# Moving the transposed activations and branch outputs by 32 bytes modulo 256 in a hybrid decoder trunk

## The chip, the core and the metric

The kernel runs on one core of a Trainium2 chip. The metric is device time in microseconds of one execution. TensorE (PE) multiplies, with a separate weight-load stream (PEld); VectorE (DVE), ScalarE (ACT) and GpSimd (POOL) do the elementwise work; SyncE (SP) issues most transfers.

## The reference

Two layers. Each has a parallel mixer (an mLSTM branch and a gated DeltaNet branch, both fed by one input projection), a gated merge, an output projection and a layer norm, then a SwiGLU block and a second layer norm. Everything is float32, with 256 tokens and a model width of 1024.

```python
proj = einsum('bsd,dn->bsn', x, w_in)              # q, k, v, gates of both branches
ha = mlstm(...) ; hb = gated_delta(...)            # 4 heads of 128/256, 8 heads of 128
y = sigmoid(gate_a) * (ha @ w_branch_a) + sigmoid(gate_b) * (hb @ w_branch_b)
x = layernorm(ALPHA * x + y @ w_out)
gt, up = split(x @ w_ffn_up)                       # 2 x 2816 columns
x = layernorm(ALPHA * x + (silu(gt) * up) @ w_ffn_down)
```

## The kernel before

**Precision and matmuls.** Every large product is made from three float32r matmuls: each operand is held as a high part and a remainder (`xtH`/`xtL` for the activations, two halves of one tile for the weights), and high x high, high x low and low x high are summed in PSUM (`three`, L281; L304; L324). One instruction, `mm` at L279, issues them all, so the trace knows them by tile names. In an `out<-a,b` of L279 the moving operand (streamed) is the first of the two where the row has 256 columns and `xtH`, `xtL`, `haH` and so on lead; with 512 columns the weights move and the activations are loaded.

**Two forms.** `chunkB` (L377) loads a 128 x 128 block of the weight unit (`wR`) and streams 256 columns of the transposed activations; `chunkA`, `pairA` and `splitA` (L296, L312, L335) load a 128 x 128 block of the activations and stream 512 columns of the weight unit. The last pass of the last layer (`pieces=2`, L1172) streams weights in halves of 256 columns. Before each matmul stands its own weight load: 7,474 matmuls, 7,474 loads.

**Weight units.** Weights arrive in units of 128 x 1024 floats. `loading` (L233) puts a unit's high and low part side by side in one of six ring buffers `wR` (`SLOT` floats each, L49), or in a spot that is free for a while (`wT0` to `wT3`, `wh0` to `wh2`; `SPOTS`, L45). ACT makes the high part (L255), DVE the remainder (L256). `SHIFT` (L50) moves a unit inside its ring buffer; the units listed at L166 (va, oa, zb, up0, up1 and, in the last layer, dn1 from its fifth unit on, where they have no spot of their own) are shifted, the rest lie at its start.

**Where the operands lie.** The pools hand out addresses in the order in which tiles are made. Byte address in a partition modulo 256, from the built program:

| tile | role | modulo 256 |
|---|---|---|
| `xtH`, `xtL` | transposed activations | 128 |
| `haH`, `haL`, `hbH`, `hbL` | transposed outputs of the two branches | 128 |
| `wR`, unshifted; `wT*`, `wh*` | weight units | 192 |
| `wR`, shifted by 48 floats | weight units of the 512-column form | 128 |
| `yH`, `yL`, `hH`, `hL` | merged branches; SwiGLU activations | 192 |
| `wgH`, `wgL` | gate weights, 24 columns (96 bytes) for each of 8 blocks | 128 + 96 k |

Column slices are multiples of 512 bytes, so these hold for every matmul of a kind; for the gates the block k decides. In what follows the **offset** of a pair is the address of the loaded operand minus that of the streamed one, modulo 256: 64 for `xt`, `ha`, `hb` streamed against an unshifted unit, 0 where a shifted unit is streamed against `xt`, 0 for `yH` and `hH` with an unshifted unit or a spot, minus 64 where a spot is streamed against `xt`, and 64 where the shifted units of dn1 meet `hH`.

**Order.** PE's order is written out by hand (`PLAN`, L125: U is one unit of large matmuls, the other words are pieces of the branches). The other engines' order comes from a list scheduler in the file (`arrange`, L1217) with costs of its own, which knows no addresses.

Of the kernel before, what the change touches and what calls it, by code (L numbers as in the profile page):

```python
# [12 lines left out]
F32 = mybir.dt.float32  # L13
# [4 lines left out]
P = 128  # L18
# [19 lines left out]
def chunk_order():  # L38
    return ORDER + ["wb", "wo"] + [f"up{j}" for j in range(UP)] + ["dn0", "dn1"]
# [7 lines left out]
         ("va0", 0): "T0", ("va0", 1): "T1", ("va0", 2): "T2", ("va0", 3): "T3"}  # L47
WARM = 8
SLOT = 2 * UC + 64  # L49
SHIFT = 48  # L50
STEPS = (1, 4, 7, 10, 14, 18, 23, 30)
LN_LATE = (5, 6)
LATE = 8 * (UP - 3)
# [84 lines left out]
class Net:  # L138
    def __init__(self, ctx, tc, a, dbg=None):
        self.tc, self.nc, self.a, self.dbg = tc, tc.nc, a, dbg  # L140
        nc = tc.nc
        self.fix = ctx.enter_context(tc.tile_pool(name="fix", bufs=1))
        self.raw = ctx.enter_context(tc.tile_pool(name="raw", bufs=4))
        self.hl = ctx.enter_context(tc.tile_pool(name="hl", bufs=6))
        self.pj = ctx.enter_context(tc.tile_pool(name="pj", bufs=4, space=bass.MemoryType.PSUM))
        self.sm = ctx.enter_context(tc.tile_pool(name="sm", bufs=4, space=bass.MemoryType.PSUM))
        self.dr = ctx.enter_context(tc.tile_pool(name="dr", bufs=2, space=bass.MemoryType.DRAM))
        self.u = 0
        self.clock = 0
        self.due = []  # L150
        self.lnt = {}
        self.ahead = []
        self.ring = 0
        self.busy = set()
        self.F = None
        self.t3 = False
        self.spots = {}
        self.shift = {}
        n = 0
        for l in range(NL):  # L160
            for name in chunk_order():
                for i in range(COUNT.get(name, 4)):
                    spot = SPOTS.get((name, i))
                    if spot and (name != "va0" or l):
                        self.spots[n] = spot
                    elif name[:2] in ("va", "oa", "zb") or name in ("up0", "up1") or l == NL - 1 and name == "dn1" and i > 3:  # L166
                        self.shift[n] = SHIFT
                    n += 1
        fix = self.fix
        self.xt = [fix.tile([P, KT, S], F32R, name="xtH"), fix.tile([P, KT, S], F32R, name="xtL")]  # L170
        self.cst = fix.tile([P, 4 * P + 2 * S], F32, name="cst")
        c = self.cst
        self.idn = c[:, 0:P]
        self.tri = c[:, P:2 * P]
        self.one = c[:, 2 * P:3 * P]
        self.gm = c[:, 3 * P:4 * P]
        self.pm = c[:, 4 * P:4 * P + S]
        self.ei = c[:, 4 * P + S:4 * P + 2 * S]
        self.x = fix.tile([P, 2, D], F32, name="x")
        self.mh = fix.tile([P, 8], F32, name="mh")  # L180
        self.ph = fix.tile([P, 8], F32, name="ph")
        nc.gpsimd.memset(self.mh, -0.5)
        nc.gpsimd.memset(self.ph, 0.5)
        nc.vector.memset(self.x[:, 0, 0:P], 0.0)
        ps = self.sm.tile([P, 512], F32, name="sm")
        for i in range(WARM):
            self.mm(ps[:, 0:P], self.x[:, 0, 0:P], self.x[:, 0, 0:P], True, True)
# [758 lines left out]
    def mixer(self, l):  # L946
        nc, M, a = self.nc, self.M, self.a
        xt = self.xt
        mt = M.tile
# [9 lines left out]
            nc.gpsimd.memset(t, 0.0)  # L959
        st = [{}, {}]  # L960
        sm = {}
        self.gnc = mt([P, 16], F32, name="gnc")[:, 0:1]
        gates = self.gates(l, xt)
        cw = mt([P, 24, 4], F32, name="cw")
        self.gn = gn = mt([P, D], F32, name="gn", tag="vs", bufs=2)
# [447 lines left out]
```

## Time and profile before

| | us |
|---|---|
| median of three runs (1019.75 to 1020.79) | 1020.4 |
| the profiled execution | 1020.09 |
| its span, first to last instruction | 1018.3 |
| PE busy | 1006.9 |
| DVE busy | 734.8 |
| ACT busy | 595.6 |

An entry of the grouped views reads: line, engine, operation, out<-in tiles, shape, count, busy time, mean nanoseconds of one. Matmuls overlap: one of 256 columns lasts some 276 ns in its record while the next starts some 113 ns later. The distance from start to start is the pace that PE pays; the duration shows which pace a stretch ran at.

### The profile page before, as it was taken

How to read it: one execution, taken by the hardware profiler on the slowest of the kernel's cores; microseconds unless marked ns; L12 is line 12 of the kernel's file. 1: busy time of each engine (PE TensorE's matmuls, PEld its weight loads, DVE VectorE, ACT ScalarE, POOL GpSimd, SP SyncE). 2: the span in 40 equal slices, each digit the busy share in tenths (PEclk: the TensorE clock that was granted, in tenths of full speed). 3: DMA queues.
4: the chain of work that ended last, by engine and by line, in shares of the span. 5: the costliest groups of instructions: out<-in, count | busy, mean ns of one | idle time of the engine just before them, and what ended most of it. 6: DMA issues, size and time to landing. Idle time of an engine off the chain costs nothing.

```text
span 1018.3 us, 18926 instructions
## 1 busy us (share of the span) xinstructions
PE 1006.9 (99%) x7474; PEld 941.1 (92%) x7474; DVE 734.8 (72%) x1311; ACT 595.6 (58%) x1108; POOL 45.4 (4%) x68
## 2 busy tenths in 40 slices
PE   9999999999999999999999999999999999999997
PEld 7999999999998899998889999998999989999886
DVE  5788998799668655556647799878994885556453
ACT  5677567866655554455445865767667564445440
POOL 1000000100001000000010100001000010000001
PEclk9999999999999999999999999999999999999998
DMA  8876235645556666667644842555355666666641
GB/s 295 275 245 190 79 106 187 207 125 166 166 187 220 214 187 194 199 182 226 215 119 151 272 147 81 190 165 167 104 173 180 224 199 200 200 191 189 185 164 41
DMA packets 57400, 183.61 MB, mean 180 GB/s; under 512 B 6624, under 2 KB 14048, under 8 KB 56672
## 3 DMA queue, kind: packets, MB, share of 16 engines
q1 hardware_dynamic: 50688, 179.13, 54.7%
q10 hardware_dynamic: 6624, 3.28, 1.2%
q8 instruction: 58, 0.95, 0.4%
q14 instruction: 30, 0.25, 0.1%
HBM read 181.21 MB, written 1.18 MB: 179 GB/s over the span
## 4 chain that ended last, share of the span: by engine, by line
PE 85%; DVE 8%; ACT 3%; DMA 2%; issue 1%; POOL 0%; SPq 0%; POOLq 0%; DVEq 0%; ACTq 0%
PE pj L279 76%; PE sm L279 6%; DVE wR L256 2%; DMA raw<-in_ws 2%; DVE stt L784 1%; DVE tmp L782 1%; DVE cv L680 1%; ACT wR L255 1%; PE sm L412 1%; PE sm L695 1%; DVE wt L599 0%; ACT dg L772 0%; DVE ha L628 0%; POOL sq L624 0%; ACT KQ L718 0%
## 5 line engine op out<-in xcount | busy, mean ns | idle before, releaser
L256 DVE TENSOR_TENSOR wR<-raw,wR 128x1024 fp32r<-128x1024 f32 (+1 forms) x302 | 364.8, 1215 | 185.3 <-ACT wR L255 183.6
L279 PE MATMUL pj<-xtH,wR 128*128 128x256 f32 x2656 | 471.4, 279 | 0.0
L255 ACT CAST wR<-raw 128x1024 fp32r<-128x1024 f32 (+1 forms) x302 | 314.9, 1044 | 223.6 <-PE pj L279 173.6
L279 PEld LDWEIGHTS pj<-xtH,wR 128*128 128x128 f32 x2656 | 406.7, 188 | 0.9
L279 PE MATMUL pj<-xtL,wR 128*128 128x256 f32 x1328 | 368.6, 278 | 0.0
L279 PEld LDWEIGHTS pj<-xtL,wR 128*128 128x128 f32 x1328 | 249.9, 188 | 0.2
L279 PE MATMUL pj<-wR,xtH 128*128 128x512 f32 x432 | 124.9, 395 | 0.4 <-ACT wR L255 0.2
L279 PEld LDWEIGHTS pj<-wR,xtH 128*128 128x128 f32 x432 | 79.9, 189 | 17.7 <-ACT wR L255 1.2
L279 PE MATMUL pj<-wR,hH 128*128 128x512 f32 (+1 forms) x336 | 95.4, 369 | 0.0
L279 PE MATMUL pj<-wR,xtL 128*128 128x512 f32 x216 | 71.7, 392 | 0.0
L279 PEld LDWEIGHTS pj<-wR,hH 128*128 128x128 f32 x336 | 60.7, 188 | 10.6
L279 PE MATMUL pj<-wR,hL 128*128 128x512 f32 (+1 forms) x168 | 61.9, 369 | 0.0
L680 DVE SCALAR_TENSOR_TENSOR cv<-cu,cw,cv 128x255 f32<-128x255 f32 (+2 forms) x144 | 59.7, 476 | 2.8 <-ACT cv L678 2.6
L279 PEld LDWEIGHTS pj<-wR,xtL 128*128 128x128 f32 x216 | 40.8, 189 | 9.0
L279 PE MATMUL pj<-haH,wR 128*128 128x256 f32 x256 | 46.5, 282 | 0.0
L279 PE MATMUL pj<-hbH,wR 128*128 128x256 f32 x256 | 45.8, 280 | 0.0
L279 PEld LDWEIGHTS pj<-haH,wR 128*128 128x128 f32 x256 | 39.6, 188 | 0.0
L279 PEld LDWEIGHTS pj<-hbH,wR 128*128 128x128 f32 x256 | 39.3, 188 | 0.0
L782 DVE TENSOR_TENSOR tmp<-Mt,stt 128x248 f32<-128x248 f32 (+30 forms) x124 | 36.0, 290 | 2.9
L784 DVE TENSOR_TENSOR stt<-stt,tmp 128x248 f32<-128x248 f32 (+30 forms) x124 | 35.9, 289 | 2.8
L279 PEld LDWEIGHTS pj<-wR,hL 128*128 128x128 f32 x168 | 31.6, 188 | 5.4
L279 PE MATMUL pj<-haL,wR 128*128 128x256 f32 x128 | 35.8, 280 | 0.0
(250 smaller groups left out, 1210.3 us busy)
## 6 DMA issues: line engine op xcount, KB each, us to landing
raw<-in_ws SPq DMA_DIRECT2D x322, 512.0 KB, 4.1
lnp<-in_ln SPq DMA_DIRECT2D x4, 1024.0 KB, 6.2
KQ<-rw ACTq DMA_DIRECT2D x8, 256.0 KB, 7.8
raw<-in_ws SPq DMA_DIRECT2D x4, 256.0 KB, 4.4
gn<-in_gn SPq DMA_DIRECT2D x2, 512.0 KB, 5.3
x<-in_x SPq DMA_DIRECT2D x1, 1024.0 KB, 8.6
mr<-rw ACTq DMA_DIRECT2D x4, 256.0 KB, 9.1
xraw<-in_xt SPq DMA_DIRECT2D x1, 512.0 KB, 8.2
```

The lines of the kernel that those rows point to most:

```text
L255: nc.scalar.copy(out=h[:, sl], in_=r[:, sl])
L256: nc.vector.tensor_sub(out=lo[:, sl], in0=r[:, sl], in1=h[:, sl].bitcast(F32))
L279: self.nc.tensor.matmul(out, lhsT=l, rhs=r, start=start, stop=stop)
L412: self.nc.tensor.transpose(ps[:, i * P:(i + 1) * P], in_=src[:, i * P:(i + 1) * P], identity=self.idn)
L680: nc.vector.scalar_tensor_tensor(out=c[:, i, s:], in0=u[:, i, 0:S - s], scalar=cw[:, t, 3 - s:4 - s], in1=c[:, i, s:], op0=ALU.mult, op1=A ...
L695: self.nc.tensor.transpose(ps[:, h * P:h * P + P], in_=src[:, h, c * P:c * P + P], identity=self.idn)
L782: nc.vector.tensor_tensor(out=tmp[:, j + 1:, :], in0=mt[:, j + 1:, j:j + 1].to_broadcast([P, n, 8]), in1=stt[:, j:j + 1, :].to_broadcast([ ...
L784: nc.vector.tensor_tensor(out=stt[:, j + 1:, :], in0=stt[:, j + 1:, :], in1=tmp[:, j + 1:, :], op=ALU.subtract)
```

## The change

`SHIFT` grows from 48 to 56 floats (32 bytes). The small constant tile `mh` (32 bytes) is made before `xt` and not after `x`, so `xtH`, `xtL`, the constants `cst` and the residual `x` lie 32 bytes further, and all that follows `mh`'s old place lies where it was. `gnc` grows from 64 to 96 bytes, and as the third of the tiles that open the mixer's pool behind `dm`, `TT`, `YY` it pushes every later mixer tile, `haH`, `haL`, `hbH`, `hbL` among them, 32 bytes further.

```diff
-SHIFT = 48
+SHIFT = 56
...
         fix = self.fix
+        self.mh = fix.tile([P, 8], F32, name="mh")
         self.xt = [fix.tile([P, KT, S], F32R, name="xtH"), fix.tile([P, KT, S], F32R, name="xtL")]
...
         self.x = fix.tile([P, 2, D], F32, name="x")
-        self.mh = fix.tile([P, 8], F32, name="mh")
         self.ph = fix.tile([P, 8], F32, name="ph")
...
-        self.gnc = mt([P, 16], F32, name="gnc")[:, 0:1]
+        self.gnc = mt([P, 24], F32, name="gnc")[:, 0:1]
```

On every engine the instructions stand in the same order as before, and none is added or taken away. What differs is addresses modulo 256, from the two built programs:

| pair (streamed, loaded) | columns | matmuls | offset before | offset after |
|---|---|---|---|---|
| `xt`, `ha`, `hb` with `wR` or `wh` | 256 | 4,800 | 64 | 32 |
| shifted `wR` with `xt` | 512 | 648 | 0 | 0 |
| `wT`, `wh` with `xt` | 512 | 120 | -64 | -32 |
| shifted `wR` of dn1 with `hH`, `hL` | 512 and 256 | 24 and 48 | 64 | 32 |
| unshifted `wR` or spots with `yH`, `yL`, `hH`, `hL` | 512 and 256 | 630 and 84 | 0 | 0 |
| `xt` with `wg`, block k | 256 | 48 | 96 k | 96 k |

## Rows read from the trace of the kernel before

**Rows 1.** The page: busy time of each engine, and PE's granted clock in tenths.
```profile
PE 1006.9 (99%) x7474; PEld 941.1 (92%) x7474; DVE 734.8 (72%) x1311; ACT 595.6 (58%) x1108; POOL 45.4 (4%) x68
...
PEclk9999999999999999999999999999999999999998
```

**Rows 2.** The page: shares of the chain that ended last.
```profile
PE 85%; DVE 8%; ACT 3%; DMA 2%; issue 1%; POOL 0%; SPq 0%; POOLq 0%; DVEq 0%; ACTq 0%
PE pj L279 76%; PE sm L279 6%; DVE wR L256 2%; DMA raw<-in_ws 2%; DVE stt L784 1%; DVE tmp L782 1%; DVE cv L680 1%; ACT wR L255 1%; PE sm L412 1%; PE sm L695 1%; DVE wt L599 0%; ACT dg L772 0%; DVE ha L628 0%; POOL sq L624 0%; ACT KQ L718 0%
```

**Rows 3.** Groups of PE by shape, whole span: count, busy us, mean ns, idle.
```profile
L279 PE MATMUL pj<-xtH,wR 128*128 128x256 f32 x2656 | 471.4, 279 | 0.0
L279 PE MATMUL pj<-xtL,wR 128*128 128x256 f32 x1328 | 368.6, 278 | 0.0
L279 PE MATMUL pj<-haH,wR 128*128 128x256 f32 x256 | 46.5, 282 | 0.0
L279 PE MATMUL pj<-hbH,wR 128*128 128x256 f32 x256 | 45.8, 280 | 0.0
L279 PE MATMUL pj<-wT,xtH 128*128 128x512 f32 x48 | 14.9, 392 | 0.0
```

**Rows 4.** The same groups, 349 to 437 us.
```profile
L279 PE MATMUL pj<-xtH,wR 128*128 128x256 f32 x501 | 85.6, 276 | 0.0
```

**Rows 5.** The same groups, 34.8 to 42.7 us.
```profile
L279 PE MATMUL pj<-xtH,wR 128*128 128x256 f32 x46 | 8.2, 281 | 0.0
```

**Rows 6.** PE in order of time near 400 us: start us, us, operation, count.
```profile
399.79 0.28 PE L279 MATMUL pj<-xtL,wR 128*128 128x256 f32 x1
...
400.81 0.28 PE L279 MATMUL pj<-xtL,wR 128*128 128x256 f32 x1
```

**Rows 7.** PE in order of time, 33 to 36 us.
```profile
33.74 0.28 PE L279 MATMUL pj<-xtL,wR 128*128 128x256 f32 x1
...
34.06 0.30 PE L483 MATMUL sm<-cst,gf 24*128 24x24 f32 x2
34.29 0.38 PE L279 MATMUL pj<-xtH,wR 128*128 128x256 f32 x1
34.51 0.28 PE L279 MATMUL pj<-xtL,wR 128*128 128x256 f32 x1
...
35.92 0.28 PE L279 MATMUL pj<-xtL,wR 128*128 128x256 f32 x1
```

**Rows 8.** PE in order of time, dn1 of layer 1, from 981 us.
```profile
981.52 0.40 PE L279 MATMUL pj<-wR,hH 128*128 128x256 f32 x2
...
982.24 0.40 PE L279 MATMUL pj<-wR,hH 128*128 128x256 f32 x2
```

**Rows 9.** Groups by shape, 1004 to 1005.6 us.
```profile
L279 PE MATMUL pj<-wR,hH 128*128 128x256 f32 x11 | 2.0, 276 | 0.0
```

**Rows 10.** Groups by shape, 995.2 to 1000.6 us, and 308.3 to 314 us.
```profile
L279 PE MATMUL pj<-wR,hH 128*128 128x512 f32 x16 | 5.0, 394 | 0.0
...
L279 PE MATMUL pj<-wR,yH 128*128 128x512 f32 x10 | 3.1, 389 | 0.0
```

**Rows 11.** Gate matmuls about 29.7 us (block 3): count, min/median/max ns, first and last start.
```profile
L279 PE MATMUL sm<-xtH,wgL x1: 280/280/280, 29.4 to 29.4; 128*24 128x256 f32 x1
...
L279 PE MATMUL sm<-xtH,wgH x1: 279/279/279, 29.5 to 29.5; 128*24 128x256 f32 x1
L279 PE MATMUL sm<-xtL,wgH x1: 276/276/276, 29.6 to 29.6; 128*24 128x256 f32 x1
```

**Rows 12.** Gate matmuls about 30.7 us (block 6), the same columns.
```profile
L279 PE MATMUL sm<-xtH,wgL x1: 277/277/277, 30.4 to 30.4; 128*24 128x256 f32 x1
...
L279 PE MATMUL sm<-xtH,wgH x1: 280/280/280, 30.6 to 30.6; 128*24 128x256 f32 x1
L279 PE MATMUL sm<-xtL,wgH x1: 278/278/278, 30.7 to 30.7; 128*24 128x256 f32 x1
```

**Rows 13.** PE in order of time: the last such matmuls of layer 1.
```profile
949.65 0.28 PE L279 MATMUL pj<-xtL,wR 128*128 128x256 f32 x1
```

## The prediction

> **What bounds the kernel now.** I read the page's busy times first: PE is busy 1006.9 of 1018.3 us, DVE 734.8, ACT 595.6, and PE's clock is granted in full in all slices but the last [rows 1]. The chain that ended last says the same from the end: 85% of it is PE, 76% the large matmuls of L279 [rows 2]. So nothing is waited for on the whole; the kernel is as long as PE's stream of matmuls, and a change that only moves addresses can matter in one place, the pace of that stream.
>
> So the next view is the groups by shape. The 256-column matmuls have mean durations of 277 to 282 ns [rows 3], and the means hide two values. Between 349 and 437 us 501 of them have a mean of 276 [rows 4]; between 34.8 and 42.7 us the same instruction with the same offset has 281 [rows 5]. In order of time the first kind starts nine matmuls in 400.81 - 399.79 = 1.02 us, 113.3 ns each [rows 6]; the second starts twelve in 35.92 - 34.51 = 1.41 us, 117.5 ns each [rows 7]. Call them the fast and the slow pace, 4.2 ns apart. A stretch keeps its pace until something else comes between: the one in [rows 7] ran fast until the small transposes at 34.06, and slow from then on. At offset 0 there is a third pace: streamed weights in halves, dn1 of layer 1, six starts in 982.24 - 981.52 = 0.72 us, 120 ns each [rows 8]. The same form on shifted units (offset 64) is back at 276 [rows 9]. With 512 columns it is the other way round: 389 ns at offset 0, 394 at offset 64 [rows 10]. The two operands' addresses modulo 256 therefore do set PE's pace, and offset 64 with 256 columns has two stable answers.
>
> By single records, 1,559 of the 4,854 matmuls of 256 columns at offset 64 (six of the gates among them) last 279 to 284 ns, 3,213 last 274 to 278, and the other 82 are longer, nearly all next to a restart. The first long stretch at 117.5 ns stands in [rows 7], the last ends in [rows 13].
>
> **The change part by part.** No instruction is added, removed or moved on any engine, nor on any DMA queue; no wait is added. What is left:
>
> - *4,800 matmuls of 256 columns go from offset 64 to 32.* This is the whole question. The trace of before has no long stretch at 32. Bounds from rows: below, every one of the slow pace takes the fast pace, 1,559 x 4.2 = 6.5 us less. Above, all run at the pace of offset 0: 3,241 x 6.7 + 1,559 x 2.5 = 25.6 us more. The nearest row is in the gates, whose loaded blocks lie at 128 + 96 k against `xt` at 128: block 3 has offset 32, with 24 loaded columns in place of 128. While its loads ran, three successive matmuls lasted 280, 279 and 276 ns [rows 11]: a collision that resolves itself at the third. Block 6 has offset 64: 277, 280, 278 [rows 12]; it does not resolve in three. So at 32 the stream seems to slide out of the slow pace, at 64 it can stay in it. I take that, most of the slow stretches gone. Some slow matmuls must stay: there are about 76 restarts by small matmuls, and if each costs three at the slow pace, 76 x 3 = 228 remain. Worth: (1,559 - 228) x 4.2 = 5.6 us.
> - *120 matmuls of 512 columns go from -64 to -32.* Now at 392 against 389 ns [rows 3, 10]: 120 x 3 = 0.4 us less at best; if they went to the 394 of offset 64, 0.2 more. I take 0.2 less, half way to offset 0.
> - *72 matmuls of dn1 go from 64 to 32.* The 24 wide ones are at 394 and could reach 389: 0.1 us less. The 48 halves are at 276 and could go to the 283 of offset 0: 0.3 more. I take nothing.
> - *768 matmuls of 512 columns with shifted units* keep offset 0, both operands 32 bytes further. At residue 192 [the `yH` pair of rows 10] they run at 389, as those at 128 do at best; nothing is taken. The small float32 matmuls of the branches are hidden in the same stream and have durations of their own; a few pairs (`kq1`, `hb`, `ha` against the constants) change offset: some 200 instructions by at most the 2 to 4 ns between any two paces above, under 1 us either way, taken as zero.
> - *Transfers and elementwise work* at the new addresses: DVE and ACT have 28% and 42% of the span free [rows 1], which covers a change of some per cent in any one instruction; PE waits for neither in the long stretches of [rows 4].
>
> Sum: 1020.1 - 5.6 - 0.2 = 1014.3 us for the profiled execution; its time stands 0.3 us under the median, so 1014.6 on the median's scale.
>
> **A rule that speaks against the change.** The durations of [rows 4, 5, 8] differ for one and the same shape, and the one thing that differs between [rows 8] and [rows 9] is the offset. The Trainium skill, page "TensorE: Matmul & The Clock Gate", section "Step-by-step: what each phase is for", says that PE has two independent read ports and that loading the next weights takes no read bandwidth from the running matmul. By that rule no offset would matter and the time would stay at 1020.4; the trace does not agree (283 against 276 ns).
>
> **The rivals.**
>
> *More of the slow pace.* Offset 32 lies half way between 0, where nearly all halves run at 120 ns, and 64, where a third run at 117.5. If the penalty simply falls with distance, 32 is worse than 64. With the slow share doubled, 1,559 x 4.2 = 6.5 us more, 1026.9; with all slow, 3,241 x 4.2 = 13.6 us more, 1034.0. The place is the long stretches of [rows 4] (501 matmuls in that row alone, and as many in layer 1), which are fast now and would turn slow; the change loses as soon as more than a third of the 4,800 are slow. For it: the pace of [rows 8], and that the first gate matmul at 32 is as long as any at 64. Against it: the gate rows end fast.
>
> *The pace of offset 0 everywhere*, because 32 bytes is too little to part the two streams, or because a streamed operand that starts at 160 in place of 128 costs a step per matmul. 4,800 at 120 ns or worse: 25.6 us more, 1046. For it: no streamed float32r operand of before starts at a residue that is not a multiple of 64. Against: the third matmul of [rows 11].
>
> *Nothing to speak of.* The slow share is set by the restarts and not by the offset, and comes out within some 450 matmuls of 1,559: 1020.4 within 2 us. The two paces at one offset speak for it [rows 4, 5]; a third pace at offset 0 speaks against [rows 8].
>
> **How the numbers follow.** Less of the slow pace: 0.44, at 1014.6, with its own range from 1013.0 (nothing left at the slow pace, and the 0.4) to 1018.3. About the same: 0.14. More of the slow pace: 0.30, from 1022.5 to 1034.0. The pace of offset 0 or worse: 0.12, near 1046. The likeliest single case is the first. The range reaches down to 1012.8 and up to 1034.0, so that all but the last case and the rims are in it, about 0.86. A measurement of this kernel can tell about 0.2% (2 us) from no change: faster 0.44, same 0.14, slower 0.42. The two signs are nearly even, because the one row at offset 32 is a short load and the neighbours on either side disagree with it.
>
> **What would show it.** In the profile after, the group `pj<-xtH,wR` with 256 columns: a mean of 276 to 277 over the span proves the forecast, 281 the first rival, 283 the second, 279 the third. The stretch after the small transposes at 34 us should fall back to 276 within a few matmuls. 349 to 437 us must stay at 276; if it turns slow the forecast is lost. The shifted 512-column group should keep its mean, and the counts, the order and DVE's and ACT's means should be as before. Wrong would be above all the step from three short gate loads to 4,800 full ones.

## The result and the profile after

The change makes the kernel slower: 1035.8 us (median, 1035.2 to 1035.9) against 1020.1 us for the kernel before on the same chip, a ratio of 1.015 with a 95% interval of 1.0137 to 1.0164. The prediction was 1014.6, in a range that ended at 1034.0.

The page of the kernel after shows the same work, with PE busier by as much as the span has grown (1034.1 against 1018.3 us):

```profile
PE 1022.8 (99%) x7474; PEld 957.1 (93%) x7474; DVE 735.3 (71%) x1311; ACT 597.1 (58%) x1108; POOL 45.3 (4%) x68
...
PE 94%; DVE 4%; ACT 1%; DMA 1%; SPq 0%; issue 0%; POOL 0%; POOLq 0%; DVEq 0%; ACTq 0%
```

PE has 15.9 us more, DVE 0.5, ACT 1.5 [rows 1], and PE's part of the chain that ended last has grown from 85% to 94% [rows 2]. The groups by shape over the whole span (count, busy us, mean ns, idle) say which matmuls took it:

```profile
L279 PE MATMUL pj<-xtH,wR 128*128 128x256 f32 x2656 | 485.5, 283 | 0.0
L279 PE MATMUL pj<-xtL,wR 128*128 128x256 f32 x1328 | 373.1, 281 | 0.0
...
L279 PE MATMUL pj<-hbH,wR 128*128 128x256 f32 x256 | 47.4, 284 | 0.0
L279 PE MATMUL pj<-haH,wR 128*128 128x256 f32 x256 | 47.1, 283 | 0.0
...
L279 PE MATMUL pj<-wT,xtH 128*128 128x512 f32 x48 | 15.1, 395 | 0.0
```

Against [rows 3] the 256-column matmuls are longer by 4, 3, 4 and 1 ns, and the 48 wide ones from a spot by 3. The place is the one the first rival named, the stretch that ran entirely at 276 ns before [rows 4]. Between 349 and 437 us the same group now has

```profile
L279 PE MATMUL pj<-xtH,wR 128*128 128x256 f32 x463 | 82.3, 281 | 0.0
```

and in order of time, near 400 us (start us, us, operation, count):

```profile
399.48 0.28 PE L279 MATMUL pj<-xtL,wR 128*128 128x256 f32 x1
...
401.26 0.28 PE L279 MATMUL pj<-xtL,wR 128*128 128x256 f32 x1
```

Fifteen starts lie between these two: 1.78 us / 15 = 118.7 ns each, where [rows 6] had 113.3. By single records, the 4,618 matmuls of this form that directly follow one another start 118.3 ns apart on average, 114.8 before; 3.5 x 4,618 = 16.2 us, which covers the whole difference of 15.8 us. Before, 113 and 114 were two thirds of them; after, the shortest distance is 115, and the distances repeat a pattern from 115 to 123 ns, the same near 60, 360 and 860 us. At offset 32 there is no fast pace.

The same records show how sharply the two paces were parted before. Restarts and other matmuls cut the 256-column matmuls into 71 unbroken stretches. Apart from the first few matmuls of a stretch, 39 of them run at the fast pace and 32 at the slow one, and none changes on the way.

### The profile page after: what moved, and what is told of

Read it like the earlier page. It is cut to its first block, busy times and chain, and to the rows that moved or that the text cites. A ratio compares the mean times of both kernels' runs of the same rounds, so it can differ in the third digit from the quotient of the medians.

```text
span 1034.1 us, 18926 instructions
## 1 busy us (share of the span) xinstructions
PE 1022.8 (99%) x7474; PEld 957.1 (93%) x7474; DVE 735.3 (71%) x1311; ACT 597.1 (58%) x1108; POOL 45.3 (4%) x68
## 4 chain that ended last, share of the span: by engine, by line
PE 94%; DVE 4%; ACT 1%; DMA 1%; SPq 0%; issue 0%; POOL 0%; POOLq 0%; DVEq 0%; ACTq 0%
PE pj L279 84%; PE sm L279 7%; PE sm L412 1%; PE sm L695 1%; DVE wR L256 1%; DVE tmp L782 1%; DVE stt L784 1%; DMA raw<-in_ws 1%; DVE cv L680 0%; ACT wR L255 0%; DVE wt L599 0%; DVE ha L628 0%; POOL sq L624 0%; PE sm L1145 0%; SPq L254 0%
## 5 line engine op out<-in xcount | busy, mean ns | idle before, releaser
L279 PE MATMUL pj<-xtH,wR 128*128 128x256 f32 x2656 | 485.5, 283 | 0.0
L279 PEld LDWEIGHTS pj<-xtH,wR 128*128 128x128 f32 x2656 | 411.6, 188 | 0.9
L279 PE MATMUL pj<-xtL,wR 128*128 128x256 f32 x1328 | 373.1, 281 | 0.0
L279 PE MATMUL pj<-hbL,wR 128*128 128x256 f32 x128 | 36.0, 281 | 0.0
```

The lines of the kernel that those rows point to most:

```text
L279: self.nc.tensor.matmul(out, lhsT=l, rhs=r, start=start, stop=stop)
```

## Experiments

Each was made from one kernel by the edit shown, and is compared with the kernel before on the same chip. Theory O: the offset of the loaded to the streamed operand sets the pace, pair by pair. Its rivals: the absolute start of the streamed operand (160) costs; the mixer's other tiles cost. Open as well was what had gone wrong in the step from the gates.

### Offset 32 without moving the activations, and half of the change

```diff
+UNITS = 56
...
                         self.shift[n] = SHIFT
+                    elif name[:2] not in ("wo", "dn"):
+                        self.shift[n] = UNITS
```

> The kernel before, with the unshifted units of the 256-column matmuls (and no other tile) laid 56 floats into their ring buffer, so that loaded minus streamed address is 32 modulo 256 as after the change, while xt, ha and hb still start at 128. If the offset of the two operands alone sets the pace: as after the change, 1035.8 us, and a mean of 283 ns for the 256-column group of xtH. If instead the streamed operand's start at 160 in place of 128 costs it: as before, 1020.1 us and 279 ns.

Measured: 1035.3 us, ratio 1.015 (1.0133 to 1.0166). The groups with `wR` are those of the change to the nanosecond, with `xt`, `ha`, `hb` still at 128 (the 48 matmuls with a unit in the spot `wh1` keep offset 64):

```profile
L282 PE MATMUL pj<-xtH,wR 128*128 128x256 f32 x2656 | 485.4, 283 | 0.0
...
L282 PE MATMUL pj<-hbH,wR 128*128 128x256 f32 x256 | 47.4, 284 | 0.0
L282 PE MATMUL pj<-haH,wR 128*128 128x256 f32 x256 | 47.1, 283 | 0.0
```

So it is the offset alone. Where the tiles lie, the vector work and the transfers at new addresses cost nothing that can be measured here.

The change without its last line (`gnc` stays at 16 floats):

```diff
-        self.gnc = mt([P, 24], F32, name="gnc")[:, 0:1]
+        self.gnc = mt([P, 16], F32, name="gnc")[:, 0:1]
```

> The change without its last line: xt, the constants and the shifted units move, the mixer's tiles and so ha and hb stay (offset 64). If each matmul pays by its own pair, 4,032 of the 4,800 pay: 15.7 x 4,032 / 4,800 = 13.2 us more than before, 1033.3 us, with ha and hb at 280 to 282 ns and xt at 283. If the cost lay with the small matmuls and vector work of the mixer, little of it would show here.

Measured: 1033.4 us, ratio 1.013 (1.0115 to 1.0145), 13.4 us more than before where 13.2 was worked out. The groups split as they should: `xt` as after the change, `ha` and `hb` no longer.

```profile
L279 PE MATMUL pj<-xtH,wR 128*128 128x256 f32 x2656 | 485.4, 283 | 0.0
...
L279 PE MATMUL pj<-hbH,wR 128*128 128x256 f32 x256 | 45.8, 280 | 0.0
L279 PE MATMUL pj<-haH,wR 128*128 128x256 f32 x256 | 45.8, 280 | 0.0
```

### The three gate rows, made 24

The prediction took from three gate matmuls that at offset 32 a collision resolves itself [rows 11]. This kernel pads the blocks so that all 24 of a layer have that offset; the two gate tiles use buffers that are free at that time.

```diff
-        wH = M.tile([P, KT * 24], F32R, name="wgH", tag="tmp")
-        wL = M.tile([P, KT * 24], F32R, name="wgL", tag="dg")
+        wH = M.tile([P, KT, 64], F32R, name="wgH", tag="H")[:, :, GATE:GATE + 24]
+        wL = M.tile([P, KT, 64], F32R, name="wgL", tag="C")[:, :, GATE:GATE + 24]
```

> The kernel before, with only the gate weights laid out anew: each block of 24 columns begins 256 bytes after the one before, at 160 modulo 256, so that all 24 gate matmuls of a layer (not three) run at offset 32. The prediction rested on three of them ending at 276 ns. If offset 32 does settle with short loads, and only full loads of 128 columns do not: 280, 279, 276 at the most and then 276 to the end, mean 276 to 277 ns. If the three rows were too few: the 24 go on between 278 and 283 ns, as the full loads after the change do.

Measured, min/median/max ns of the gate matmuls of both layers:

```profile
L280 PE MATMUL sm<-xtH,wgH x16: 281/281/281, 28.8 to 534.8; 128*24 128x256 f32 x16
L280 PE MATMUL sm<-xtL,wgH x16: 280/280/280, 28.9 to 535.0; 128*24 128x256 f32 x16
L280 PE MATMUL sm<-xtH,wgL x16: 280/280/281, 29.0 to 535.1; 128*24 128x256 f32 x16
```

Not one of them settled: offset 32 by itself does not lead out of the slow pace. What gave [rows 11] its 276, where each block comes at another offset than the one before, stays open. The contrast between [rows 11] and [rows 12] also hangs on how records and blocks are paired. The prediction took the three matmuls that run while a block is loaded, so that each group begins with the last matmul of the block before. The three that use the block, which is the pair that the offset is defined by, end in the kernel before with

```profile
L279 PE MATMUL sm<-xtH,wgL x1: 276/276/276, 29.8 to 29.8; 128*24 128x256 f32 x1
...
L279 PE MATMUL sm<-xtH,wgL x1: 276/276/276, 30.8 to 30.8; 128*24 128x256 f32 x1
```

for block 3 and block 6. So block 3 reads 279, 276, 276 and block 6, at offset 64, reads 280, 278, 276: both reach 276, and the contrast between an offset that resolves and one that does not is gone.

The same run shows a second thing. Behind the gates come full loads at offset 64; from 31.8 to 34.2 us in this kernel, and from 31.4 to 33.8 us in the kernel before:

```profile
L280 PE MATMUL pj<-xtH,wR 128*128 128x256 f32 x15 | 2.8, 281 | 0.0
```
```profile
L279 PE MATMUL pj<-xtH,wR 128*128 128x256 f32 x15 | 2.7, 276 | 0.0
```

Same instructions, same offset, 281 against 276 ns, and the same again in layer 1: at offset 64 what ran before a stretch decides its pace. Here the gates' 281 goes on. It is not simply the last matmul's duration that is carried on: in the kernel before, the last three gate matmuls lasted 281, 277 and 279 ns by single records, and the stretch behind them is fast from the start. The time of the one run of this kernel, 1020.4 us, is as before; both kernels fall into the slow pace at the next restart, behind the small transposes of [rows 7].

### The other offsets

The edit of the first experiment with other numbers of floats. Each ratio is to the kernel before on the same chip, where its median was 1019.9 to 1020.1 us.

> The same edit with 16 floats: offset 128. If the penalty falls with the distance from 0 modulo 256 and nothing else, 128 is the best of all offsets: all 256-column matmuls at 276 ns, 1020.1 - 6.5 = 1013.6 us. If the period is 128 bytes, it is as bad as offset 0: 4,750 matmuls at 120 ns, about 1045 us. The gate block at offset 128 (three matmuls of 276 ns) speaks for the first, but short loads have misled once.

> The same edit with 32 floats: offset 192, which is -64. If only the distance counts, it is as 64: 1020 us with both paces. If it counts which operand is ahead, it differs from 64 by more than 2 us either way; the 512-column matmuls at -64 (392 ns against 394 at +64) speak for a little less than at 64.

> The kernel before with the unshifted units of the 256-column matmuls 8 floats further: offset 96. Offsets 32 and 128 cost 15 and 17 us, 64 and 192 keep the pace of 113 ns in part of the kernel. If 64 modulo 128 is what matters and 32 to either side is out of reach: like 32, 1035 us and 283 ns, no stretch at 276. If the penalty rises only towards 0 and 128: between, 1022 to 1030 us.

> The same edit with 4 floats: offset 80, 16 bytes past 64. If the good place is a window round 64, this is inside: both paces as now (1020 us) or, if the window has an end without the slow pace, 1014 us. If it is 64 exactly: slow throughout, about 1030 to 1035 us.

> The same edit with 60 floats: offset 48, 16 bytes short of 64. If the good place is a window round 64: 1014 to 1020 us, and then the side on which the slow pace is rarer shows which way the window lies. If it is 64 exactly: slow throughout, about 1030 to 1035 us.

> The kernel before with the unshifted units of the 256-column matmuls 2 floats further: offset 72, 8 bytes past 64. 48, 80 and 96 cost 17 us. If what counts is 64 to the byte: again 1037 us, no stretch at 276 ns. If the two streams meet in lines of 16 bytes, 72 lies in the same line as 64: both paces, about 1020 us.

> The same edit with 62 floats: offset 56, 8 bytes short of 64. If 64 to the byte counts: about 1037 us. If lines of 16 bytes count, 56 lies in the line of 48: about 1038 us as well, while offset 72 is near 1020 us. If a narrow window round 64 counts, both 56 and 72 are near 1020 us.

| offset of the 256-column pairs | us | ratio to before, 95% interval |
|---|---|---|
| 32 (the change) | 1035.8 | 1.015, 1.0137 to 1.0164 |
| 48 | 1037.8 | 1.0173, 1.0158 to 1.0189 |
| 56 | 1032.8 | 1.0127, 1.0112 to 1.0142 |
| 64 (before) | 1020.1 | |
| 72 | 1035.1 | 1.015, 1.0133 to 1.0167 |
| 80 | 1037.3 | 1.017, 1.0153 to 1.0187 |
| 96 | 1036.9 | 1.0166, 1.015 to 1.0181 |
| 128 | 1037.0 | 1.0165, 1.015 to 1.0181 |
| 192 | 1025.6 | 1.0054, 1.0039 to 1.0069 |

The theories that let the penalty fall with distance from 0 are out: 128 is as bad as 32. A window round 64 would have to be narrower than 8 bytes to either side: these cost 12.7 us on one side and 14.9 on the other. Only 64 and 192 keep the fast pace over a stretch; by single records, at the other seven no two distances in succession are at 114 ns or less, the unit in the spot left out. From 349 to 437 us, offset 128, offset 96 and offset 192:

```profile
L282 PE MATMUL pj<-xtH,wR 128*128 128x256 f32 x456 | 81.3, 281 | 0.0
```
```profile
L282 PE MATMUL pj<-xtH,wR 128*128 128x256 f32 x459 | 82.7, 283 | 0.0
```
```profile
L282 PE MATMUL pj<-xtH,wR 128*128 128x256 f32 x491 | 83.6, 276 | 0.0
```

At 192 the slow pace of 117.5 ns follows restarts more often than at 64, which is its 5.5 us: 7 of the 71 stretches are fast, the two longest among them, against 39 before, and 64% of the matmuls start 116 to 119 ns apart, against a third. The Trainium skill, page "SBUF — State Buffer", section "Specifications (TRN2)", gives lines of 16 bytes. If the line of the loaded operand decided, offset 72, which lies in the line of 64, should do as well. It does not (1035.1 against 1020.1 us), so the line is not what decides.

### Two tries at a better version

> A try at less of the slow pace: in the unshifted units of the 256-column matmuls the low part lies 32 floats further, so that of three loads two are at offset 64 and one at 192. Both offsets keep a pace of 113 ns once it is there. If the slow pace at 64 needs three like loads in a row, it ends within a few matmuls of each restart: 1014 to 1016 us, xtH at 276 to 277 ns. If it only needs 64 modulo 128: 1020 to 1026 us. If a change of offset from load to load costs by itself: over 1030 us.

```diff
                         self.shift[n] = SHIFT
+                    elif name[:2] not in ("wo", "dn"):
+                        self.apart[n] = 32
...
-            h, lo = hold[:, at:at + UC], hold[:, at + UC:at + 2 * UC]
+            lo = at + UC + self.apart.get(self.u, 0)
+            h, lo = hold[:, at:at + UC], hold[:, lo:lo + UC]
```

Measured: 1015.7 us, ratio 0.9962 (0.9949 to 0.9975): faster than both kernels. The groups over the whole span:

```profile
L283 PE MATMUL pj<-xtH,wR 128*128 128x256 f32 x2656 | 467.3, 278 | 0.0
L283 PE MATMUL pj<-xtL,wR 128*128 128x256 f32 x1328 | 367.0, 276 | 0.0
```

and the same restart as in [rows 7], in order of time:

```profile
33.87 0.30 PE L487 MATMUL sm<-cst,gf 24*128 24x24 f32 x2
34.09 0.38 PE L283 MATMUL pj<-xtH,wR 128*128 128x256 f32 x1
34.31 0.28 PE L283 MATMUL pj<-xtL,wR 128*128 128x256 f32 x1
...
35.69 0.28 PE L283 MATMUL pj<-xtL,wR 128*128 128x256 f32 x1
```

The twelve matmuls from 34.31 to 35.69 take 1.38 us where [rows 7] has 1.41; the first two are long (120 and 118 ns by single records), and from then on the distance is 113.3. The slow pace still follows restarts, but it no longer lasts: by single records the longest run of distances over 114 ns is 12 matmuls, where before it was 118. The mean of 278 ns for `xtH` (276 to 277 was expected) still holds these and the long first matmuls of the stretches. By single records the mean distance is 113.7 ns against 114.8 before: 1.1 x 4,618 = 5.1 us, a little more than the 4.4 us measured.

> The same with whole units: every second unit of the 256-column matmuls lies at offset 192, the others at 64, so the offset changes every 24 matmuls. If a change from one to the other ends the slow pace: at most 24 slow matmuls after a restart, about 1015 us. If it is carried over: between the kernel before and offset 192 throughout, 1020 to 1026 us. If the change can also start the slow pace: the long stretches at 350 and 850 us turn slow in part, over 1026 us.

```diff
                         self.shift[n] = SHIFT
+                    elif name[:2] not in ("wo", "dn") and n % 2:
+                        self.shift[n] = 32
```

Measured: 1020.2 us, ratio 1.0001 (0.9992 to 1.0011). That is two effects against each other. Between 54.5 and 68 us the group still has

```profile
L281 PE MATMUL pj<-xtH,wR 128*128 128x256 f32 x64 | 11.7, 282 | 0.0
```

so the slow pace can be carried over when the offset changes from one unit to the next. But it can also end there. From 37.7 to 42.7 us, the later part of the stretch of [rows 5], this kernel and the kernel before have

```profile
L281 PE MATMUL pj<-xtH,wR 128*128 128x256 f32 x31 | 5.4, 276 | 0.0
```
```profile
L279 PE MATMUL pj<-xtH,wR 128*128 128x256 f32 x30 | 5.3, 281 | 0.0
```

The stretch begins slow, and its first change from 192 to 64 turns it fast. With the offset of each matmul taken from the built program and set beside its record, the slow pace ended at 14 of 21 changes from 192 to 64 that it met, and at none of 15 from 64 to 192; no change turned a fast stretch slow. Against that stands that 48 of the 71 stretches begin slow, where it was 32 before, and these two cancel. The low part at 192 of the kernel above makes a change from 192 to 64 in every three matmuls, which fits its short slow runs; that this is the reason was not tested by itself.

## Why the prediction was wrong

- **What bounds the kernel** was right: PE's stream, and in it the pace. All of the 15.8 us lies in the group that was named, and order, counts and the other engines are as before.
- **The step that failed is the choice of the value at offset 32.** It was taken from three gate rows, "the stream seems to slide out of the slow pace". With 24 such matmuls in a row none does (280 to 281 ns in all of them), and with full loads none does either: the offset alone, in the first experiment, gives 118.3 ns and 1035.3 us. Nor did the gate rows hold the contrast with 64: paired by the block that a matmul uses, block 3 and block 6 both end at 276 ns. A sequence in which the offset changes every three matmuls does not show what a constant offset does; the step from short loads to full ones, named as the weak one, was not the culprit, since the short loads at a constant 32 are slow too.
- **The first rival came true, with its size a little short.** It gave 1034.0 for all slow, at the 117.5 ns of offset 64. Offset 32 has a pace of its own, 118.3 on average, so the upper end of the range was 1.8 us too low. Its reason, a penalty that falls with distance, was wrong: 96 and 128 are no better. The sign it was to be known by failed as well: the `xtH` group shows 283 ns, which was the sign of the second rival, while its pace is 118.3 and not 120. A mean duration that stood for a pace at one offset does not stand for it at another.
- **The upper bound, 120 ns everywhere (1046)**, held: the worst offset tried, 48, is at 1037.8. That a start at 160 costs a step per matmul is refuted by the first experiment, where no streamed operand starts there and the time is the same.
- **The third rival** (the offset matters little, restarts decide) is wrong for 32, and for 192 too: the restarts there are the same, and the slow share is twice that of 64. What is right in it is that at either offset a restart is where the pace is settled.
- **The smaller terms.** The 120 wide matmuls from spots were to gain 0.2 us; they went to 395 ns, some 0.4 us lost. The shifted 512-column pairs and the float32 matmuls of the branches were taken as nothing: the first experiment, which leaves them where they were, has the same time within 0.5 us. Two slips in the working move nothing: with shifted units 648 matmuls of 512 columns keep offset 0, not 768 (the table of the change), and 6.5 and 0.4 off 1020.4 make the lower end 1013.5, not 1013.0.
- **The rule against the change**, which the prediction quotes from the Trainium skill, page "TensorE: Matmul & The Clock Gate", section "Step-by-step: what each phase is for", says that loads take no read bandwidth from the running matmul. By it the time was to be 1020.4 for any offset. The runs disagree: with nothing moved but the units, the times go from 1020.1 at offset 64 to 1037.8 at 48.

What the runs don't settle is the mechanism under the offset: why 64 modulo 128 has a pace of 113.3 ns and 8 bytes to the side have none, and why a change from 192 to 64 often ends the slow pace and one from 64 to 192 does not. The last was seen in the alternating kernel and tried in no other.

## What to carry to other kernels

Where float32r matmuls load new weights for each 256 columns, the addresses of the loaded and the streamed tile relative to each other were worth some 2% here (1015.7 to 1037.8 us). Sweep them finely, by shifting one of the two inside its buffer, before any larger layout change; which offsets win in another kernel was not tried. Read the pace from starts in order of time, not from mean durations, which hide two paces and do not compare across offsets. A total that stays the same can hold two effects that cancel, as in the alternating kernel: look at the stretches one by one. A price taken from a few rows needs the same neighbours before and after as the place where it will be used; where these differ, make a small kernel that repeats the case.

## What was not expected of the hardware

- At offset 64 a stretch keeps its pace, 113.3 or 117.5 ns, to its end: none of the 71 stretches of the kernel before changed after its first few matmuls. What ran just before decides which: behind the gates 281 or 276 ns, by how the gates were laid out.
- Of nine offsets only 64 and 192 hold 113.3 ns per 256 columns; 56 and 72 are at 1032.8 and 1035.1 us.
- One load in three at the other of the two good offsets removed four fifths of the slow distances (1,543 to 306 over 114 ns) and 4.4 us, with no instruction added or taken away. The same two offsets alternating by unit gained nothing: 14 stretches turned fast on the way, but 16 more began slow.
